# A two-layer decoder on one core: the second weight row's sum moved into an accumulating DMA, and the squared-ReLU tiles handled in pairs

## The chip, the cores and the metric

The kernel runs on one core of one Trainium2 chip. The metric is the device time of one execution in microseconds (us), as the median of several runs. Before the change it is 2010.63 us over three runs, from 2010.59 to 2010.78.

## The reference

Two layers work on `x` of 256 tokens by 2048 channels, in float32. Each layer has a token mixer (causal pooling in layer 0, differential attention in layer 1) beside a memory cross-attention, an output projection, and then the block that the change touches, a squared-ReLU MLP over 8192 hidden channels:

```python
def squared_relu_mlp(h, w1, w2):
    z = jax.nn.relu(h @ w1)          # w1: 2048 x 8192
    return (z * z) @ w2              # w2: 8192 x 2048

    # in each layer i:
    x = x + jnp.concatenate([token_out, mem_out], axis=-1) @ w_out[i]
    x = x + squared_relu_mlp(rms_norm(x, ffn_norm[i]), w_ff1[i], w_ff2[i])
```

## The kernel before

**Split products.** Every weight is read from memory in float32 and split on the chip into a high part, rounded to the type that TensorE takes (`hi_ring`, a cast by ScalarE, L178), and the rest (`lo_ring`, a subtraction by VectorE, L181). Activations are split in the same way. A product of two split matrices takes three products of the parts; the one of the two rests is left out. `hi_ring` and `lo_ring` are rings of six slots of 512 columns, so the splits can be only a few blocks ahead of TensorE.

**The order of loading and splitting.** The program runs twice. The first, dry pass writes down the order in which weights are used; `Plan.close` makes of it the list of preparations (`prep`) and the list of loads. Class `Feed` then loads rows of 1024 columns through SyncE's queue (`load`, L122) and splits jobs up to three ahead of the one in use (`_prepare`, L190). A job `N` is a plain block of 512 columns. A job `S` belongs to a slab of ff2.

**The MLP** (`ffn`, L730). 64 tiles of ff1 (`up_tile`, 128 hidden channels each) are made one after the other in one PSUM bank, `x_bank`. Each is evicted, its two halves are added, then ReLU, square and split follow. Two neighbouring tiles and 1024 columns of ff2 make a slab: a 2 by 2 by 2 block product, computed with seven products in place of eight (a fast scheme for 2 by 2 matrices). 60 slabs in each layer are computed between the ff1 tiles, in four jobs `S0` to `S3` each (`slab_jobs`, `product`, L862); `due` fixes how many jobs come before which tile. The last eight slices of ff1 go into eight tiles of the output in plain form (`down_tile`).

The scheme needs sums on both sides. On the side of the activations, VectorE builds four sums of 128 columns for each pair (L792 to L795), which are split in a buffer of their own (`sit`, L800 and L803), beside the four original blocks (`z`, L772 and L776). On the side of the weights, with the slab's two rows called r0 and r1, each of two halves:

- `t1` = left half of r0 + left half of r1. A plain DMA brings the first, an accumulating DMA that GpSimd issues (L153) adds the second in flight (`first_sum`).
- Step `K`, first of the slab: VectorE makes r1's left half = `t1` - r1's right half (L204). Only the right half of r1 is loaded (L143).
- `S0` splits r0, `S1` splits `t1`, `S2` splits r1; behind the split of `S0`, VectorE turns both halves of r0 into differences (L218, 1024 columns), and `S3` splits those.

r0 and r1 of a slab with an even number lie in a pool of three tiles (`rows`), r1 of an odd one in `spare`, a part of `room`. So a tile is loaded again only when the split that reads it, two slabs before, has been done.

**Order on the engines.** Within what the program writes, a scheduler puts the instructions of each engine in a fixed order, and each engine works through its own in that order: an instruction that waits holds up all behind it on its engine.

Of the kernel before, what the change touches and what calls it, by code (L numbers as in the profile page):

```python
# [55 lines left out]
class Plan:  # L56
# [13 lines left out]
    def close(self):  # L70
        prep = []
        for job in self.jobs:

            if job[0] == "S" and job[2] == 0:
                prep.append(("K", job[1]))
            prep.append(job)
# [4 lines left out]
        for p in prep:  # L81
            if p[0] == "K":
# [16 lines left out]
class Feed:  # L99
# [22 lines left out]
    def load(self, upto):  # L122
        while self.lp < min(upto, len(self.plan.loads)):
# [18 lines left out]
            else:  # L142
                self.nc.sync.dma_start(t[:, 512:1024], self.wst[h, :, 512:1024])  # L143
# [46 lines left out]
    def _prepare(self, p):  # L190
        sub, add = self.nc.vector.tensor_sub, self.nc.vector.tensor_add
# [11 lines left out]
        if p[0] == "K":  # L203
            one = sub(rb[:, 0:512], t1, rb[:, 512:1024])  # L204
# [10 lines left out]
        if p[2] == 0:  # L215
            t2 = rb[:, 0:512].unsqueeze(1).to_broadcast([P, 2, 512])
            two = ra.rearrange("p (a c) -> p a c", a=2)
            sub(two, t2, two)  # L218
        if p[2] == 1:
            self.t1_of[p[1] % len(self.t1)] = None  # L220
        if p[2] == 3:
# [70 lines left out]
def program(ctx, tc, plan, dry, xT, memT, par, lam, cst, wst, yT):  # L292
# [437 lines left out]
    def ffn(l, xs, tags, done):  # L730
# [7 lines left out]
        z = sp.tile([P, NK, 512], F32R, tag=tags[0], name=f"z{l}")  # L738
        room = sp.tile([P, 8192], F32, tag=tags[1], name=f"room{l}")
        sums_in = sp.tile([P, 4, 1024], F32R, tag="big", name=f"sit{l}")  # L740
        staged = sp.tile([P, 2048], F32, tag="big2", name=f"stage{l}")
        sit = [sums_in[:, j, :] for j in range(4)]
        stage = [staged[:, T * j : T * j + T] for j in range(8)]
        sums = [room[:, 512 * j : 512 * j + 512] for j in range(2)]
        feed.t1 = [room[:, 1024 + 512 * j : 1536 + 512 * j] for j in range(3)]
        outs = [room[:, 2560 + 512 * j : 3072 + 512 * j] for j in range(2)]
# [7 lines left out]
        z_done, sit_done = set(), set()  # L754
        z_free = {j: True for j in range(NK)}
        sit_free = [True] * 4

        def evict(ps):
            x = outs[cnt[0] % 2]
            cnt[0] += 1  # L760
            return x, nc.scalar.copy(x, ps)  # L761
# [4 lines left out]
        def convert(j):  # L766
            a = stage[j % 8]
            k = j % NK

            def high():  # L770
                z_free[k] = False
                nc.scalar.copy(z[:, k, 0:T], a)  # L772
                at(1, low)

            def low():
                nc.vector.tensor_sub(z[:, k, T : 2 * T], a, z[:, k, 0:T].bitcast(F32))  # L776
                z_done.add(j)

            when(lambda: z_free[k], high)
            if j % 2 == 0:  # L780
                return
            i = j // 2

            def ready():
                return j in z_done and j - 1 in z_done and sit_free[i % 4]

            def combine():
                sit_free[i % 4] = False
                a11, a21 = stage[2 * i % 8][:, 0:P], stage[2 * i % 8][:, P:T]
                a12, a22 = stage[(2 * i + 1) % 8][:, 0:P], stage[(2 * i + 1) % 8][:, P:T]  # L790
                s1, s2, s3, s4 = (sums[i % 2][:, c * P : c * P + P] for c in range(4))
                nc.vector.tensor_add(s1, a21, a22)  # L792
                nc.vector.tensor_sub(s3, a11, a21)
                nc.vector.tensor_sub(s2, s1, a11)
                nc.vector.tensor_sub(s4, a12, s2)  # L795
                at(1, sums_high)
                at(2, sums_low)

            def sums_high():
                nc.scalar.copy(sit[i % 4][:, 0:512], sums[i % 2])  # L800

            def sums_low():
                nc.vector.tensor_sub(  # L803
                    sit[i % 4][:, 512:1024], sums[i % 2], sit[i % 4][:, 0:512].bitcast(F32)
                )
                sit_done.add(i)

            when(ready, combine)

        def up_tile(i, ps, between=None):  # L810
# [5 lines left out]
            y, out = evict(ps)  # L816
            if i == 3 and not dry:
                feed.cast_behind = [out.ins.name] * 3
            at(1, lambda: nc.vector.tensor_add(y[:, 0:T], y[:, 0:T], y[:, T : 2 * T]))
            d = 5 if i == 2 else 2  # L820

            def relu():
                one = nc.scalar.activation(y[:, 0:T], y[:, 0:T], AF.Relu)
                if i == 2 and not dry:
                    feed.order(one, feed.last_cast.ins.name)

            at(d, relu)

            def square():
                assert i < 8 or i - 8 in z_done  # L830
                nc.scalar.activation(stage[i % 8], y[:, 0:T], AF.Square)
                at(1, lambda: convert(i))

            at(d, square, 2)

        def down_tile(n, ps, between=None):
            ks = range(56, 64)
            assert all(k in z_done for k in ks)
            if n >= 3:
                c_tile(ps, "w_ff2", l, n, ks, z)  # L840
# [5 lines left out]
            a_part(ps, "w_ff2", l, n, ks, z, between=between)  # L846
            x, _ = evict(ps)
# [24 lines left out]
        def slab_jobs(g, i, again, end):  # L872
# [9 lines left out]
            def plain(c, t):  # L882
                assert k + c in z_done
                zk = z[:, (k + c) % NK, :]
# [753 lines left out]
```

## Time and profile before

| | |
|---|---|
| median of 3 runs | 2010.63 us (2010.59 to 2010.78) |
| span of the profiled execution | 2010.7 us |
| TensorE busy | 1999.0 us, 99% |
| VectorE busy | 1779.2 us, 88% |
| ScalarE busy | 1525.3 us, 76% |
| GpSimd busy | 157.1 us, 8% |
| TensorE's mean granted clock | 0.999 |
| moved by DMA | 422.19 MB, 210 GB/s |

The profile is of one execution. PE is TensorE's matmuls, PEld its weight loads, DVE VectorE, ACT ScalarE, POOL GpSimd, SP SyncE. A row of a group of instructions gives the line, the engine, the operation, the names written and read, shapes and count, then the busy time in us and the mean of one in ns, then the idle time of the engine just before them. A row of waits gives who waited for whom, in us in total, times, and the longest. A row of a window gives its length, and for each engine the busy time with the count of instructions, then the granted clock of TensorE, the share of the DMA engines' time that packets took, and GB/s. The MLP of layer 0 lies at about 257 to 931 us of the span, that of layer 1 at 1336 us to the end.

### The profile page before, as it was taken

To read this page: it belongs to the slowest core of one execution; us is meant where nothing else is said; L and a number is where in the kernel's file an instruction comes from. 1 tells how busy PE (TensorE), PEld (TensorE's weight loads), DVE (VectorE), ACT (ScalarE), POOL (GpSimd) and SP (SyncE) were. 2 spreads that over 40 slices of the span, in tenths; PEclk is the share of its full clock that TensorE was granted. 3 is DMA by queue.
4 is the path that set the end of the run, shared out by engine and by line. 5 is a ranking of instruction groups with operands and counts; after the bars stand their busy time and mean duration, and the time that the engine had idled before them with its cause. 6 is when DMAs were issued, how large, how long until landed. Compare 5 with 4: busy or idle time off the path is not lost.

```text
span 2010.7 us, 31966 instructions
## 1 busy us (share of the span) xinstructions
PE 1999.0 (99%) x10510; PEld 1696.5 (84%) x10510; DVE 1779.2 (88%) x3096; ACT 1525.3 (76%) x2838; POOL 157.1 (8%) x187
## 2 busy tenths in 40 slices
PE   9999999999999999999999999999999999999999
PEld 8888888888888888888888888888888888888877
DVE  8888888989999999999765698878989999999998
ACT  7765577787887888878665699557787878878885
POOL 0001310000000000100000000320000000100000
PEclk9999999999999999999999999999999999999999
DMA  8555576777778777755575533567777777777773
GB/s 319 171 188 195 188 221 208 232 221 229 226 226 240 223 218 234 225 175 175 181 235 194 178 127 126 199 197 229 224 214 233 225 234 223 231 230 231 223 228 124
DMA packets 145030, 422.19 MB, mean 210 GB/s; under 512 B 16352, under 2 KB 19040, under 8 KB 144864
## 3 DMA queue, kind: packets, MB, share of 16 engines
q1 hardware_dynamic: 127440, 388.69, 57.5%
q0 software_dynamic: 17280, 31.46, 9.7%
q8 instruction: 82, 1.34, 0.3%
q14 instruction: 84, 0.69, 0.1%
q10 hardware_dynamic: 144, 0.01, 0.0%
HBM read 418.00 MB, written 2.10 MB: 209 GB/s over the span
## 4 chain that ended last, share of the span: by engine, by line
PE 93%; ACT 3%; DVE 2%; issue 1%; DMA 0%; ACTq 0%; DVEq 0%
PE x_bank L433 21%; PE x_bank L435 11%; PE p L867 9%; PE p L870 9%; PE p L869 9%; PE wo L433 6%; PE wo L435 3%; PE u L433 2%; ACT hi_ring L178 1%; PE ff L433 1%; PE u L435 1%; PE k L469 1%; PE q L467 1%; PE q L469 1%; PE q L468 1%; PE v L468 1%
## 5 line engine op out<-in xcount | busy, mean ns | idle before, releaser
L178 ACT CAST hi_ring<-raw 128x512 fp32r<-128x512 f32 x969 | 593.5, 623 | 267.3 <-PE x_bank L433 61.1
L181 DVE TENSOR_TENSOR lo_ring<-raw,hi_ring 128x512 fp32r<-128x512 f32 x969 | 662.0, 695 | 105.1 <-ACT hi_ring L178 93.5
L433 PE MATMUL x_bank<-fx,hi_ring 128*128 128x512 f32 x1952 | 610.8, 394 | 0.0
L435 PEld LDWEIGHTS x_bank<-fx,lo_ring 128*128 128x128 f32 x1952 | 365.1, 188 | 88.1 <-DVE lo_ring L181 6.1
L181 DVE TENSOR_TENSOR lo_ring<-slab,hi_ring 128x1024 fp32r<-128x1024 f32 x300 | 366.4, 1221 | 50.1 <-ACT hi_ring L178 48.8
L178 ACT CAST hi_ring<-slab 128x1024 fp32r<-128x1024 f32 x300 | 314.6, 1053 | 117.2 <-PE p L869 65.0
L435 PE MATMUL x_bank<-fx,lo_ring 128*128 128x256 f32 x1952 | 384.8, 278 | 1.5 <-DVE lo_ring L181 1.5
L433 PEld LDWEIGHTS x_bank<-fx,hi_ring 128*128 128x128 f32 x1952 | 320.7, 189 | 26.8 <-ACT room L761 1.3
L153 POOL DMA_DIRECT2D room<-in_w x120 | 104.0, 872 | 1139.7 <-DMA room<-in_w 1121.4
L867 PE MATMUL p<-hi_ring,sit 128*128 128x512 f32 x480 | 190.5, 397 | 0.4 <-ACT hi_ring L178 0.2
L869 PE MATMUL p<-hi_ring,sit 128*128 128x512 f32 x480 | 187.9, 391 | 0.0
L870 PE MATMUL p<-lo_ring,sit 128*128 128x512 f32 x480 | 186.5, 391 | 0.2
L433 PE MATMUL wo<-cat,hi_ring 128*128 128x512 f32 x512 | 161.8, 397 | 0.3 <-DVE rc L404 0.3
L181 DVE TENSOR_TENSOR lo_ring<-room,hi_ring 128x512 fp32r<-128x512 f32 x180 | 154.3, 863 | 5.7 <-ACT hi_ring L178 5.6
L178 ACT CAST hi_ring<-room 128x512 fp32r<-128x512 f32 x180 | 138.1, 769 | 19.0 <-PE p L869 9.5
L867 PE MATMUL p<-hi_ring,z 128*128 128x512 f32 x360 | 141.2, 392 | 0.7 <-ACT hi_ring L178 0.7
L869 PE MATMUL p<-hi_ring,z 128*128 128x512 f32 x360 | 140.6, 391 | 0.0
L870 PE MATMUL p<-lo_ring,z 128*128 128x512 f32 x360 | 139.7, 392 | 0.0
L435 PEld LDWEIGHTS wo<-cat,lo_ring 128*128 128x128 f32 x512 | 95.9, 188 | 22.0
L870 PEld LDWEIGHTS p<-lo_ring,sit 128*128 128x128 f32 x480 | 89.8, 188 | 21.8 <-DVE lo_ring L181 2.7
L867 PEld LDWEIGHTS p<-hi_ring,sit 128*128 128x128 f32 x480 | 90.0, 187 | 15.6 <-ACT hi_ring L178 5.8
L435 PE MATMUL wo<-cat,lo_ring 128*128 128x256 f32 x512 | 101.5, 279 | 0.0
(370 smaller groups left out, 3339.9 us busy)
## 6 DMA issues: line engine op xcount, KB each, us to landing
raw<-in_w SPq DMA_DIRECT2D x484, 512.0 KB, 4.3
slab<-in_w SPq DMA_DIRECT2D x120, 512.0 KB, 4.4
room<-in_w SPq DMA_DIRECT2D x180, 256.0 KB, 3.3
room<-in_w POOLq DMA_DIRECT2D x120, 256.0 KB, 5.7
slab<-in_w SPq DMA_DIRECT2D x60, 256.0 KB, 4.3
memraw<-in_mem SPq DMA_DIRECT2D x5, 512.0 KB, 4.5
resid<-in_x SPq DMA_DIRECT2D x8, 256.0 KB, 5.5
out_y<-resid SPq DMA_DIRECT2D x16, 128.0 KB, 1.9
```

Source lines behind the costliest of these rows:

```text
L153: self.nc.gpsimd.dma_start(self.t1[i], right, accum_op=ALU.add)
L178: self.last_cast = self.nc.scalar.copy(hi, src)
L181: low = self.nc.vector.tensor_sub(lo, src, hi.bitcast(F32))
L433: nc.tensor.matmul(ps, hi, xs[:, k, :], start=first and c == 0, stop=False)
L435: nc.tensor.matmul(ps[:, T : 2 * T], lo, xs[:, k, 0:T], start=False, stop=last and c == len(ks) - 1,)
L467: nc.tensor.matmul(ps[t], x[t][1], hi, start=k == 0, stop=False)
L468: nc.tensor.matmul(ps[t], x[t][0], hi, start=False, stop=False)
L469: nc.tensor.matmul(ps[t], x[t][0], lo, start=False, stop=k == NK - 1)
L867: nc.tensor.matmul(ps, a[1], hi, start=new, stop=False, **again)
L869: nc.tensor.matmul(ps, a[0], hi, start=False, stop=False, **again)
L870: nc.tensor.matmul(ps, a[0], lo, start=False, stop=end, **again)
```

## The change

- **Weights.** r1 is loaded whole (L143), and a second accumulating DMA of GpSimd adds its right half onto its left half. The step `K` moves from the head of the slab to behind `S1`, and is now two additions of 512 columns: r0's left half = `t1` + r1's right half, then r0's right half += that. The subtraction over 1024 columns behind `S0` goes. `t1` is set free after `S3` in place of `S1`. Nothing is subtracted any more; signs are moved into the sums of the activations and into the steps that put the seven products together (`close_left`, `finish_banks`, and the places of the banks in `of_job`).
- **Activations.** Two ff1 tiles are evicted side by side into one buffer (`two_y`). One addition, one ReLU and one square of 512 columns serve both. The square is written into a row of eight blocks of 128 columns; three VectorE operations (256, 128 and 128 columns) build the four sums in that row, and one cast and one subtraction split the seven operands that the products use (896 columns; 1024 for the last four pairs, which the plain tiles read too). Six pairs have a place (`z`, `zb`) where before there were 16 single blocks and four groups of sums.

The core of the diff:

```diff
-            if job[0] == "S" and job[2] == 0:
+            prep.append(job)
+            if job[0] == "S" and job[2] == 1:
                 prep.append(("K", job[1]))
-            prep.append(job)
...
-                self.nc.sync.dma_start(t[:, 512:1024], self.wst[h, :, 512:1024])
+                self.nc.sync.dma_start(t, self.wst[h])
+                self.nc.gpsimd.dma_start(t[:, 0:512], self.wst[h, :, 512:1024], accum_op=ALU.add)
...
         if p[0] == "K":
-            one = sub(rb[:, 0:512], t1, rb[:, 512:1024])
-            if p[1] % PER_PART:
-                self.order(one, self.last_low.ins.name)
+            one = add(ra[:, 0:512], t1, rb[:, 512:1024])
+            self.order(one, self.last_low.ins.name)
+            add(ra[:, 512:1024], ra[:, 0:512], ra[:, 512:1024])
...
-        if p[2] == 0:
-            t2 = rb[:, 0:512].unsqueeze(1).to_broadcast([P, 2, 512])
-            two = ra.rearrange("p (a c) -> p a c", a=2)
-            sub(two, t2, two)
-        if p[2] == 1:
+        if p[2] == 3:
             self.t1_of[p[1] % len(self.t1)] = None
...
+            def combine():
+                twice = block(A21).unsqueeze(1).to_broadcast([P, 2, P])
+                nc.vector.tensor_sub(
+                    block(S1, 2).rearrange("p (a c) -> p a c", a=2), twice,
+                    block(A22, 2).rearrange("p (a c) -> p a c", a=2),
+                )
+                nc.vector.tensor_sub(block(S2), block(S1), block(A11))
+                nc.vector.tensor_add(block(S4), block(A12), block(S2))
...
             def high():
-                z_free[k] = False
-                nc.scalar.copy(z[:, k, 0:T], a)
+                pair_free[i % 6] = False
+                nc.scalar.copy(pair(i)[:, 0, 0:n], u[:, 0:n])
...
-            at(1, lambda: nc.vector.tensor_add(y[:, 0:T], y[:, 0:T], y[:, T : 2 * T]))
...
+                nc.scalar.activation(left, left, AF.Relu)
+                u = staged[:, i // 2 % 2, 512:1024].rearrange("p (a c) -> p a c", a=2)
+                nc.scalar.activation(u, left, AF.Square)
```

**VectorE in the middle of the MLP of layer 0, before.** One slab: `slab_6925` is its r0, `slab_6929` its r1, `room_2604` as a source of `lo_ring` is `t1`, `raw_` rows are jobs `N`.

```order
L204 TENSOR_TENSOR slab_6929<-room_2604,slab_6929 128x512
L792 TENSOR_TENSOR room_2604<-stage_2606 128x128
L794 TENSOR_TENSOR room_2604<-room_2604,stage_2606 128x128
L795 TENSOR_TENSOR room_2604<-stage_2606,room_2604 128x128
L181 TENSOR_TENSOR lo_ring<-slab_6925,hi_ring 128x1024
L181 TENSOR_TENSOR lo_ring<-raw_6952,hi_ring 128x512
L218 TENSOR_TENSOR slab_6925<-slab_6929,slab_6925 128x1024
L181 TENSOR_TENSOR lo_ring<-room_2604,hi_ring 128x512
L181 TENSOR_TENSOR lo_ring<-slab_6929,hi_ring 128x1024
L181 TENSOR_TENSOR lo_ring<-raw_6952,hi_ring 128x512
L776 TENSOR_TENSOR z_2603<-stage_2606,z_2603 128x256
```

The same slab in the changed kernel; `slab_6777` is r0, `slab_6781` is r1.

```order
L785 TENSOR_TENSOR stage_2606<-stage_2606 128x256
L789 TENSOR_TENSOR stage_2606<-stage_2606 128x128
L790 TENSOR_TENSOR stage_2606<-stage_2606 128x128
L182 TENSOR_TENSOR lo_ring<-slab_6777,hi_ring 128x1024
L182 TENSOR_TENSOR lo_ring<-raw_6794,hi_ring 128x512
L182 TENSOR_TENSOR lo_ring<-room_2604,hi_ring 128x512
L205 TENSOR_TENSOR slab_6777<-room_2604,slab_6781 128x512
L182 TENSOR_TENSOR lo_ring<-slab_6781,hi_ring 128x1024
L207 TENSOR_TENSOR slab_6777<-slab_6777 128x512
L182 TENSOR_TENSOR lo_ring<-raw_6794,hi_ring 128x512
```

The step `K` (L204 before, L205 and L207 now) has moved from ahead of the split of r0 to behind that of `t1`, and the 1024-wide L218 is gone. The split of r1 is third of the slab's four, as before.

**GpSimd's queue, from the end of layer 0's output projection, before.** L706 and L707 are the squares of the norm, L153 the accumulating DMAs.

```order
L706 TENSOR_TENSOR psq<-resid 128x256
L707 TENSOR_TENSOR acc<-acc,psq 128x256
L153 DMA room_2604<-in_w 128x512 x60
L700 TENSOR_TENSOR acc<-resid 128x256
L706 TENSOR_TENSOR psq<-resid 128x256
```

The same place in the changed kernel: L154 is the accumulation onto `t1`, L144 that onto r1.

```order
L703 TENSOR_TENSOR acc<-acc,psq 128x256
L154 DMA room_2604<-in_w 128x512 x3
L144 DMA room_2604<-in_w 128x512
L154 DMA room_2604<-in_w 128x512
L144 DMA slab_3004<-in_w 128x512
L154 DMA room_2604<-in_w 128x512
L144 DMA room_2604<-in_w 128x512
```

The two kinds take turns in one queue, so an accumulation onto `t1` now stands behind one that waits for r1's plain load to land, and the other way round.

More of the change, by code (lines that the diff above doesn't have):

```diff
@@ L81, in close @@
         for p in prep:
-            if p[0] == "K":
+            if p[0] == "S" and p[2] == 0:
                 self.loads += [("S", p[1], 0), ("S", p[1], 1)]
@@ L753, in ffn, with pair, __getitem__ @@
         cnt = [0]
-        z_done, sit_done = set(), set()
-        z_free = {j: True for j in range(NK)}
-        sit_free = [True] * 4
+        done_pairs = set()
+        pair_free = [True] * 6
+        S1, S3, S2, S4, A12, A22, A11, A21 = range(8)
+        def pair(i):
+            i = i % 6
+            return z[:, i] if i < 4 else z_more[:, i - 4]
+        class Chunks:
+            def __getitem__(self, at):
+                _, k, c = at
+                k = 48 + k
+                half = pair(k // 2)[:, :, 512 + 256 * (1 - k % 2) : 768 + 256 * (1 - k % 2)]
+                if c == slice(None):
+                    return half
+                return half[:, 0 if c.start == 0 else 1, :]
         def evict(ps):
@@ L784, in ready @@
[L784 to L797, printed above, removed]
@@ L799, in sums_high @@
[L799 to L802 removed]
                 nc.vector.tensor_sub(
[L804 removed]
+                    pair(i)[:, 1, 0:n], u[:, 0:n], pair(i)[:, 0, 0:n].bitcast(F32)
                 )
[L806 to L808 removed]
+                done_pairs.add(i)
+            combine()
         def up_tile(i, ps, between=None):
```

109 lines of the change are left out of this document (49 added, 60 removed).

## The prediction

> **What bounds the kernel now.** I read the page first, for the engines' shares.
>
> ```profile
> span 2010.7 us, 31966 instructions
> PE 1999.0 (99%) x10510; PEld 1696.5 (84%) x10510; DVE 1779.2 (88%) x3096; ACT 1525.3 (76%) x2838; POOL 157.1 (8%) x187
> ```
>
> TensorE is busy for 99% of the span, and the change takes no product from it. So the question is how much of its time is idle where the change works. The windows answer it: the MLP of layer 0, the junction behind it, the stretch of low clock that follows, and the MLP of layer 1.
>
> ```profile
> 257.00:902.00 645.00, 643.45 (x3298) 542.27 (x3297) 598.34 (x911) 521.53 (x892) 52.06 (x60) 1.00 0.74 222
> 902.00:934.00 32.00, 29.28 (x195) 25.31 (x193) 31.39 (x64) 25.89 (x52) 0.00 (x0) 1.00 0.39 132
> 934.36:937.77 3.41, 3.41 (x10) 2.63 (x9) 2.80 (x7) 0.99 (x3) 0.00 (x0) 0.50 0.48 154
> 1336.00:1980.00 644.00, 642.67 (x3296) 541.81 (x3295) 598.08 (x910) 520.75 (x891) 51.95 (x60) 1.00 0.74 222
> ```
>
> TensorE's idle time is 645.00 - 643.45 = 1.55 us in the first MLP, 644.00 - 642.67 = 1.33 us in the second, 32.00 - 29.28 = 2.72 us in the junction. At half the clock for 3.41 us it does 1.7 us of work, so 1.7 us are lost there too. All that the change can win is the sum: 1.55 + 1.33 + 2.72 + 1.7 = 7.3 us, 0.36% of the time. The waits of TensorE in these stretches say what holds it (first MLP, junction, second MLP).
>
> ```profile
> PE x_bank L435 <- DVE lo_ring L181: 1.0, 2, 0.6
> PE p L867 <- ACT hi_ring L178: 0.3, 2, 0.2
> ```
> ```profile
> PE k L467 <- DVE room L842: 1.2, 1, 1.2
> PE k L469 <- DVE lo_ring L181: 0.7, 1, 0.7
> PE ff L449 <- DVE lo_ring L181: 0.6, 1, 0.6
> ```
> ```profile
> PE x_bank L435 <- DVE lo_ring L181: 0.8, 2, 0.6
> PE p L867 <- ACT hi_ring L178: 0.6, 3, 0.2
> ```
>
> VectorE is late 1.0 + 0.8 = 1.8 us in the MLPs, ScalarE 0.3 + 0.6 = 0.9 us (where banks are swapped). No wait there is for a DMA.
>
> Is TensorE really full? Its starts in the timeline:
>
> ```profile
> 658.47 0.40 PE L867 MATMUL p<-hi_ring,sit 128*128 128x512 f32 x1
> 658.70 0.39 PE L869 MATMUL p<-hi_ring,sit 128*128 128x512 f32 x1
> 658.93 0.39 PE L870 MATMUL p<-lo_ring,sit 128*128 128x512 f32 x1
> ```
>
> Matmuls of 512 columns start every 0.23 us and overlap; there is no gap to fill. [...] As a rival, TensorE not being full, I give it 0.01, inside the chance of faster.
>
> **The change part by part.** The rows that price it:
>
> ```profile
> L181 DVE TENSOR_TENSOR lo_ring<-slab,hi_ring 128x1024 fp32r<-128x1024 f32 x300 | 366.4, 1221 | 50.1 <-ACT hi_ring L178 48.8
> L178 ACT CAST hi_ring<-slab 128x1024 fp32r<-128x1024 f32 x300 | 314.6, 1053 | 117.2 <-PE p L869 65.0 <-PE x_bank L433 50.0 <-ACT hi_ring L178 1.4
> L218 DVE TENSOR_TENSOR slab<-slab,slab 128x1024 f32<-128x1024 f32 x60 | 73.1, 1218 | 0.0
> L831 ACT ACTIVATE stage<-room 128x256 f32<-128x256 f32 x128 | 54.0, 421 | 2.1
> L776 DVE TENSOR_TENSOR z<-stage,z 128x256 fp32r<-128x256 f32 x128 | 53.6, 419 | 4.7 <-ACT z L772 4.4
> L823 ACT ACTIVATE room<-room 128x256 f32<-128x256 f32 x128 | 53.6, 419 | 17.7 <-DVE room L819 17.2
> L819 DVE TENSOR_TENSOR room<-room 128x256 f32<-128x256 f32 x128 | 53.5, 418 | 0.1
> L772 ACT CAST z<-stage 128x256 fp32r<-128x256 f32 x128 | 52.4, 409 | 2.0
> L803 DVE TENSOR_TENSOR sit<-room,sit 128x512 fp32r<-128x512 f32 x64 | 43.8, 685 | 0.1
> L204 DVE TENSOR_TENSOR slab<-room,slab 128x512 f32<-128x512 f32 x60 | 41.1, 685 | 10.6 <-DMA room<-in_w 10.6
> L800 ACT CAST sit<-room 128x512 fp32r<-128x512 f32 x64 | 39.9, 623 | 0.7 <-DVE room L795 0.5
> L792 DVE TENSOR_TENSOR room<-stage 128x128 f32<-128x128 f32 x64 | 18.3, 286 | 5.5 <-ACT stage L831 5.5
> ```
>
> *Slab, VectorE.* Out goes 1.218 us (L218), in comes a second 512-wide addition like L204, 0.685 us: -0.53 us for each of 120 slabs, -64 us. L204's wait for the accumulating DMA, 10.6 us at the heads of the two MLPs, goes with `K`'s new place; what is late next there is `t1` at `S1`, for which no row shows a wait, so I cost this at nothing.
>
> *Pair, VectorE.* Out: 2 x 0.418 (L819), four sums of 128 columns at 0.286 (L792 and its sisters), 2 x 0.419 (L776), 0.685 (L803), together 3.50 us. In: one addition of 512 columns, 0.685, as L204; sums of 256, 128 and 128 columns, 0.418 + 2 x 0.286; a subtraction of 896 columns, three quarters of the way from 0.685 (512) to 1.221 (1024), 1.09. Together 2.76 us. 64 pairs at -0.74 us: -47 us.
>
> *Pair, ScalarE.* Out: 2 x (0.419 + 0.421 + 0.409) + 0.623 = 3.12 us. In: ReLU and square of 512 columns at 0.623 each, after the cast L800, and a cast of 896 columns between 0.623 and 1.053, 0.95. Together 2.19 us: -0.93 us, -59 us for 64 pairs. Evictions stay two for a pair.
>
> So VectorE falls from 598.34 + 598.08 = 1196 us to 1085 us of 1289 us, from 93% to 84%, ScalarE from 1042 to 983 us, from 81% to 76%. Hardly any of the 111 and 59 us lies on the path: TensorE hides them. What counts is the 1.8 us for which VectorE is late in the MLPs; I take them to go. ScalarE's 0.9 us I leave: a swap of two banks still puts four copies ahead of the next cast, and single instructions on that queue get longer (0.95 where 0.41 and 0.62 stood).
>
> *Junction.* VectorE is busy 31.39 of 32.00 us, and what the change removes lies almost all ahead of that window. What can carry over is its backlog at the window's start, of which this shows one piece:
>
> ```profile
> 902.27 1.05 ACT L178 CAST hi_ring<-room 128x1024 fp32r<-128x1024 f32 x1
> ```
> ```profile
> 904.81 1.22 DVE L181 TENSOR_TENSOR lo_ring<-room,hi_ring 128x1024 fp32r<-128x1024 f32 x1
> ```
>
> The cast ends at 903.32, its subtraction starts at 904.81: 1.5 us behind. Bounds for the junction are 0 and the whole 2.72 + 1.7 us; I take half of the backlog, -0.7 us, since the additions, scalings and splits between 905 and 934 us keep their number and TensorE still waits for the last of them. The clock's fall I leave.
>
> *The DMAs.* Each slab now loads 256 KB more through SyncE's queue and accumulates 256 KB more through GpSimd's. GpSimd's 120 more issues lie on an engine that is busy 52 us of 645, and move past each other, and the first of a layer past the squares of the norm, which come long after its load. What counts is when r1 is ready. Rows: the landing of plain loads of 512 KB (r0, L139), that of accumulations (L153), and one of the slabs whose margin is least.
>
> ```profile
> L139 SPq DMA_DIRECT2D slab<-in_w x120: 327/328/328, 81.6 to 1970.0; - x120
> ...
> DMA to landing us min/median/max: 3.1/4.4/7.5
> ```
> ```profile
> L153 POOL DMA_DIRECT2D room<-in_w x120: 856/865/1226, 257.7 to 1954.3; - x120
> ...
> DMA to landing us min/median/max: 3.6/5.7/8.0
> ```
> ```profile
> 1671.30 0.33 SPq L143 DMA_DIRECT2D slab<-in_w  x1
> ```
> ```profile
> 1683.36 1.05 ACT L178 CAST hi_ring<-slab 128x1024 fp32r<-128x1024 f32 x1 [0.58 <-PE p L869]
> ```
> ```profile
> 1684.47 0.50 PE L867 MATMUL p<-hi_ring,sit 128*128 128x512 f32 x1
> ```
>
> From the issue of r1 to its cast are 12.06 us in this slab, and TensorE takes the result at once, so nothing behind it gives way. The chain needs 4.4 + 5.7 = 10.1 us at the medians, 7.5 + 8.0 = 15.5 at the worst. If it is late, the cast `S2` waits at the head of ScalarE's queue, and behind it stand casts of ff1 blocks and evictions, then TensorE. At the medians 2 us are left, so I cost it at nothing; the upper bound is a rival.
>
> The sum: -1.8 - 0.7 + 0 = -2.5 us, a span of 2008.2 us. The runs' median is 2010.63 for a span of 2010.7, so 2010.63 - 2.5 = **2008.1 us**, -0.12%. A measurement of this kernel can tell about 0.2%, 4.0 us, from no change; so this counts as the same.
>
> **The rivals.**
>
> *The accumulation comes late (slower).* For it speaks the DMA engines' time, on the page:
>
> ```profile
> q1 hardware_dynamic: 127440, 388.69, 57.5%
> q0 software_dynamic: 17280, 31.46, 9.7%
> ```
>
> The change adds 31.46 MB to each: 9.7% once more, and 57.5 x 31.46 / 388.69 = 4.7%, together 14.4% of 2010.7 us = 289 us. All of it falls in the 1289 us of the MLPs: the share there goes from 0.74 to 0.96. If landings stretch in that proportion, the 10.1 us become 10.1 x 0.96 / 0.74 = 13.1 us, 1.0 us more than the tight slab has. At the worst landings, 15.5 us, it is 3.4 us late. A loop of r1 repeats every second slab; if half of the 60 such slabs were late by 1.0 us, that is 30 x 1.0 - 2.5, 2038 us; if a fifth, 12 x 1.0 - 2.5 = +9.5, 2020 us, which I take as its price. It decides from a chain of 12.1 us on. [...] Against it: the share counts the time that packets take while others hold them up, the same engines already move 319 GB/s in the page's first slice against 222 in the MLPs, and 62.9 MB more in 1289 us make only 271. A faster VectorE also frees r1's tile sooner. Chance 0.15.
>
> ```profile
> GB/s 319 171 188 195 188 221 208 232 221 229 226 226 240 223 218 234 225 175 175 181 235 194 178 127 126 199 197 229 224 214 233 225 234 223 231 230 231 223 228 124
> ```
>
> *The junction heals (faster).* If the whole backlog of 1.5 us carries to x_kv's splits, the junction's idle time halves, and the fall of the clock, which follows it, does not come: 1.8 + 1.4 + 1.7 = 4.9, and with ScalarE's 0.9 us 5.8 us: 2004.8 us. [...] For this rival: VectorE's load falls by a tenth. Against it: the junction's work on VectorE has as many instructions as before. Chance 0.27.
>
> *Nothing moves.* TensorE's waits could be set by the order of instructions at the swaps and heads, not by VectorE's load; longer single instructions then eat what shorter queues give. 2010.6 us. For it speaks that VectorE at 93% made TensorE wait only four times in 1289 us. Chance 0.18.
>
> **How the numbers follow.** The forecast has 0.40, and with nothing moved (0.18) makes 0.58 for the same; faster 0.27, slower 0.15. The range begins where all 7.3 us are won, 2003.3 us, and ends where nothing is won and two slabs lose the 1.0 us of the stretched chain, 2010.63 + 2.0 = 2012.6 us. Beyond it lies most of the slower rival, 0.15.
>
> **What would show it.** In the changed profile DVE should stand near 84% in the MLPs and ACT near 76%, with `x_bank <- DVE lo_ring` gone from TensorE's waits. The casts of r1 should show no wait for a DMA of `slab` or `room`; accumulations should land in 6 to 7 us. If ScalarE's `hi_ring` waits for a DMA tens of times, the slower rival has it. If no stretch of clock 0.50 follows the junction, the faster one. A gain of over 7.3 us would mean that TensorE's starts were not as full as I read them.

## The result, and the profile after

The changed kernel takes 2022.07 us, the median of four runs from 2020.88 to 2022.72; the kernel before takes 2010.70 in the same comparison. The ratio is 1.0054, with an interval from 1.0042 to 1.0066: 11.4 us slower, where 2.5 us faster was forecast and the range ended at 2012.6. The page of the changed kernel:

```profile
span 2021.0 us, 31924 instructions
PE 2000.6 (99%) x10510; PEld 1694.8 (84%) x10510; DVE 1701.0 (84%) x2842; ACT 1486.9 (74%) x2582; POOL 260.5 (13%) x307
```

TensorE does the same 10510 matmuls in a longer span, while VectorE and ScalarE have less to do, as forecast. The windows, with the columns as in the prediction (the second MLP begins 4 us later now):

```profile
257.00:902.00 645.00, 639.47 (x3270) 537.12 (x3269) 553.93 (x777) 497.53 (x758) 102.77 (x119) 1.00 0.92 269
...
1340.00:1984.00 644.00, 638.86 (x3267) 536.94 (x3267) 553.42 (x776) 497.36 (x756) 102.19 (x119) 1.00 0.92 269
```

TensorE's idle time in the MLPs has grown from 1.55 and 1.33 us to 645.00 - 639.47 = 5.53 and 644.00 - 638.86 = 5.14 us. Matmuls of 0.39 us start every 0.23 us, so part of each stall is covered by the tail of the last matmul; the whole loss is read from starts. The view of one tile gives the first and last start of each kind of matmul onto it; here the last matmul of each product (`lo_ring` by `z`) onto the banks `p`, layer 0 and layer 1, before:

```profile
L870 PE MATMUL p<-lo_ring,z x180: 389/389/497, 274.9 to 909.0; 128*128 128x512 f32 x180
```
```profile
L870 PE MATMUL p<-lo_ring,z x180: 389/389/479, 1353.5 to 1987.3; 128*128 128x512 f32 x180
```

and after:

```profile
L868 PE MATMUL p<-lo_ring,z x294: 388/389/504, 274.5 to 915.7; 128*128 128x512 f32 x147
```
```profile
L868 PE MATMUL p<-lo_ring,z x294: 389/389/505, 1357.5 to 1998.0; 128*128 128x512 f32 x147
```

The stretch of the products takes 641.2 us where it took 634.1, and 640.5 where it took 633.8: +7.1 and +6.7 us. The junction went the other way. From the last product of layer 0 to the last start on `k` (the products of `x_kv`) it was 1000.8 - 909.0 = 91.8 us:

```profile
L469 PE MATMUL k<-lo_ring,x_kv x96: 389/389/628, 929.8 to 1000.8; 128*128 128x512 f32 x96
```

and is 1004.8 - 915.7 = 89.1 us, without a stretch of low clock:

```profile
L465 PE MATMUL k<-lo_ring,x_kv x96: 389/389/497, 935.7 to 1004.8; 128*128 128x512 f32 x96
```

So 13.8 us were lost in the MLPs and 2.7 won at the junction. TensorE's waits over the whole span say for whom it stood:

```profile
PE x_bank L431 <- DVE lo_ring L182: 3.4, 4, 1.3
PE p L865 <- ACT hi_ring L179: 3.3, 8, 0.6
PE x_bank L429 <- DVE z L799: 2.3, 2, 1.2
PE p L868 <- DVE lo_ring L182: 2.3, 5, 0.6
PE x_bank L429 <- ACT hi_ring L179: 1.2, 2, 0.6
```

The wait `x_bank <- DVE lo_ring`, which was to go, has nearly doubled from 1.0 + 0.8 us, and ScalarE's has grown from 0.9 to 4.5. Followed back, there are four places.

**A late cast.** ScalarE's timeline in slab 42 of layer 0:

```profile
727.88 0.62 ACT L179 CAST hi_ring<-room 128x512 fp32r<-128x512 f32 x1
731.38 1.05 ACT L179 CAST hi_ring<-slab 128x1024 fp32r<-128x1024 f32 x1 [2.89 <-issue]
```

The idle 2.89 us are put down to "issue", to nothing that the profile ties to it. But GpSimd's timeline has the accumulation onto this r1 (L144), and the view of the DMAs its time to landing:

```profile
723.23 0.86 POOL L144 DMA_DIRECT2D slab<-in_w  x1 [8.40 <-DVE room L821]
```
```profile
slab<-in_w POOLq DMA_DIRECT2D x1, 256.0 KB, 8.1
```

It lands at 723.23 + 8.1 = 731.3 us, and the cast starts at 731.38. TensorE loses 0.54 and 0.70 us behind it. Of the 120 casts of r1, 14 start within 0.6 us of such a landing, all 14 in slabs with an even number.

**A swap of banks.** ScalarE's timeline ahead of the cast for slab 44, after and before (L916 and L924 copy banks; L827 and L829 are ReLU and square):

```profile
746.22 0.64 ACT L827 ACTIVATE room<-room 128x512 f32<-128x512 f32 x1
746.75 0.58 ACT L924 COPY room<-p 128x512 f32<-128x512 f32 x1
747.22 0.65 ACT L829 ACTIVATE stage<-room 128x512 f32<-128x512 f32 x1
747.75 0.60 ACT L916 COPY p<-room 128x512 f32<-128x512 f32 x1
...
750.26 1.07 ACT L179 CAST hi_ring<-slab 128x1024 fp32r<-128x1024 f32 x1
```
```profile
743.09 0.43 ACT L823 ACTIVATE room<-room 128x256 f32<-128x256 f32 x1
743.41 1.07 ACT L934 COPY room<-p 128x512 f32<-128x512 f32 x2
...
745.87 0.45 ACT L831 ACTIVATE stage<-room 128x256 f32<-128x256 f32 x1
746.19 0.62 ACT L926 COPY p<-room 128x512 f32<-128x512 f32 x1
```

ReLU and square stand between the same copies in both. They hold ScalarE from 746.22 to 746.75 and from 747.22 to 747.75, 1.06 us, where the single tile's held it from 743.09 to 743.41 and from 745.87 to 746.19, 0.64 us. TensorE's stall behind the cast (from start to start, above the usual distance) has grown from 0.32 to 0.74 us, by the same 0.42.

**The closing of the left half**, VectorE in slab 52 (L945 to L951 put the products together, L205 and L207 are `K`):

```profile
834.87 0.68 DVE L182 TENSOR_TENSOR lo_ring<-room,hi_ring 128x512 fp32r<-128x512 f32 x1
835.48 0.68 DVE L945 TENSOR_TENSOR room<-room,p 128x512 f32<-128x512 f32 x1
...
839.08 0.68 DVE L951 TENSOR_TENSOR room<-room,p 128x512 f32<-128x512 f32 x1
839.67 0.69 DVE L182 TENSOR_TENSOR lo_ring<-raw,hi_ring 128x512 fp32r<-128x512 f32 x1
```

Seven additions stand in a row between two splits, 4.2 us, and TensorE stalls 1.45 us for the second one (0.76 us at this place before).

**The last pair.** The chain to the first output tile of layer 0:

```profile
904.41 1.52 DVE lo_ring L182 x2
...
906.07 1.23 DVE z L799
...
907.34 0.50 PE x_bank L429
```

TensorE waits for the subtraction over all 1024 columns of the pair: 1.34 us from start to start, in layer 1 1.33. Before, no wait at these tiles was for the pair; the longest stall, 0.41 us, was for a split of weights.

### The profile page after: what moved, and what is told of

It reads as the page before. It is cut to its first block, busy times and chain, and to the rows that moved or that the text cites. A ratio compares the mean times of both kernels' runs of the same rounds, so it can differ in the third digit from the quotient of the medians.

```text
span 2021.0 us, 31924 instructions
## 1 busy us (share of the span) xinstructions
PE 2000.6 (99%) x10510; PEld 1694.8 (84%) x10510; DVE 1701.0 (84%) x2842; ACT 1486.9 (74%) x2582; POOL 260.5 (13%) x307
## 3 DMA queue, kind: packets, MB, share of 16 engines
q0 software_dynamic: 34560, 62.93, 18.4%
q8 instruction: 82, 1.34, 0.3%
## 4 chain that ended last, share of the span: by engine, by line
PE 90%; ACT 5%; DVE 3%; issue 1%; DMA 1%; DVEq 0%; ACTq 0%; POOLq 0%
PE x_bank L429 20%; PE x_bank L431 10%; PE p L868 8%; PE p L865 8%; PE p L867 8%; PE wo L429 6%; PE wo L431 3%; ACT hi_ring L179 2%; PE u L429 2%; DVE lo_ring L182 1%; PE ff L429 1%; PE u L431 1%; PE q L463 1%; PE q L465 1%; PE q L464 1%
## 5 line engine op out<-in xcount | busy, mean ns | idle before, releaser
L865 PE MATMUL p<-hi_ring,z 128*128 128x512 f32 x588 | 231.8, 394 | 2.8 <-ACT hi_ring L179 2.5
L867 PE MATMUL p<-hi_ring,z 128*128 128x512 f32 x588 | 229.9, 391 | 0.0
L868 PE MATMUL p<-lo_ring,z 128*128 128x512 f32 x588 | 227.6, 393 | 0.4 <-DVE lo_ring L182 0.4
L154 POOL DMA_DIRECT2D room<-in_w x120 | 104.5, 876 | 580.3 <-DMA room<-in_w 564.6
L144 POOL DMA_DIRECT2D slab<-in_w x60 | 51.9, 865 | 783.8 <-DVE mm_max L652 352.6
L868 PEld LDWEIGHTS p<-lo_ring,z 128*128 128x128 f32 x588 | 110.0, 188 | 29.6 <-DVE lo_ring L182 6.6
L865 PEld LDWEIGHTS p<-hi_ring,z 128*128 128x128 f32 x588 | 110.3, 188 | 20.4 <-ACT hi_ring L179 6.4
L867 PEld LDWEIGHTS p<-hi_ring,z 128*128 128x128 f32 x588 | 110.5, 188 | 13.7
L868 PE MATMUL p<-lo_ring,zb 128*128 128x512 f32 x252 | 99.7, 396 | 2.0 <-DVE lo_ring L182 1.9
```

What stands on the lines that cost most here:

```text
L144: self.nc.gpsimd.dma_start(t[:, 0:512], self.wst[h, :, 512:1024], accum_op=ALU.add)
L154: self.nc.gpsimd.dma_start(self.t1[i], right, accum_op=ALU.add)
L865: nc.tensor.matmul(ps, a[1], hi, start=new, stop=False, **again)
L867: nc.tensor.matmul(ps, a[0], hi, start=False, stop=False, **again)
L868: nc.tensor.matmul(ps, a[0], lo, start=False, stop=end, **again)
```

## The experiments

The twelve runs. "Layer 0" and "layer 1" are the stretches of the products, "junction" the time from the last product to the last start on `k`, all read as above from one profiled execution of each kernel; ratios are to the kernel before, measured beside them.

| kernel | median us | ratio and interval | layer 0 | junction | layer 1 |
|---|---|---|---|---|---|
| before | | | 634.1 | 91.8 | 633.8 |
| the change | 2022.07 | 1.0054 (1.0042-1.0066) | 641.2 | 89.1 | 640.5 |
| no_second_accumulation | 2019.49 | 1.0036 (1.0023-1.0049) | 638.6 | 89.9 | 638.1 |
| weights_part_alone | 2018.07 | 1.0029 (1.0017-1.0041) | 639.1 | 90.6 | 636.4 |
| pairs_alone | 2027.57 | 1.0078 (1.0065-1.0090) | 640.5 | 91.7 | 640.7 |
| last_pair_plain_first | 2021.73 | 1.0052 (1.0039-1.0066) | 639.6 | 91.1 | 638.3 |
| r1_loaded_first | 2019.09 | 1.0041 (1.0028-1.0054) | 638.4 | 89.5 | 638.0 |
| pair_cast_held_in_swaps | 2024.27 | 1.0067 (1.0054-1.0079) | 641.1 | 89.6 | 642.4 |
| closing_spread | 2021.33 | 1.0055 (1.0041-1.0068) | 640.8 | 89.7 | 638.9 |
| four_mended | 2013.76 | 1.0016 (1.0007-1.0025) | 634.8 | 91.4 | 635.3 |
| last_pair_only_in_layer_1 | 2012.92 | 1.0010 (1.0002-1.0019) | 636.4 | 89.0 | 634.9 |
| five_mended | 2009.29 | 0.9992 (0.9983-1.0000) | 632.5 | 92.2 | 632.7 |
| before_closing_spread | 2011.00 | 1.0001 (0.9992-1.0010) | 633.3 | 90.9 | 633.5 |
| weights_part_mended | 2005.85 | 0.9975 (0.9966-0.9985) | 632.5 | 89.9 | 631.4 |

### The parts and the late casts

**no_second_accumulation**

```diff
                 self.nc.sync.dma_start(t, self.wst[h])
-                self.nc.gpsimd.dma_start(t[:, 0:512], self.wst[h, :, 512:1024], accum_op=ALU.add)
```

> The changed kernel without the accumulating DMA onto r1 (the sum of r1's halves is left out, so the products are made of other numbers; every engine's instructions stay). Theory A, the accumulation comes late: the two MLPs lost 6.8 + 6.7 us, all because the cast of r1 waits for the DMA, so the time falls by 13 us, to about 2009. Theory B, the pair's long instructions (ReLU, square, cast and subtraction of 512 to 1024 columns in one piece) stand in front of the weight splits: no change, 2022. My own reading of the stalls lies between: the casts that follow within 0.6 us of a landing explain some 3 us of the 13, so 2019.

The stretches fall by 2.6 and 2.4 us: that is what the second accumulation costs. Theory A is left with 5 of 13.8 us, theory B is wrong as the only cause, and the reading between them, 2019, is met. Of the stalls that remain, those at slabs 28, 36, 44, 48, 49, 52 and at the last pair have the same size within 0.02 us in both layers (one of 0.34 us at slab 12 stands in layer 0 alone); those that went differ between layers and executions. That is how the two kinds are told apart here: the stalls put down to the order of instructions repeat themselves within 0.02 us, those put down to the transfers do not.

**weights_part_alone**: the kernel before with the weights part of the diff; the sums get the signs that fit it.

```diff
-                nc.vector.tensor_add(s1, a21, a22)
-                nc.vector.tensor_sub(s3, a11, a21)
+                nc.vector.tensor_sub(s1, a21, a22)
+                nc.vector.tensor_sub(s3, a21, a11)
...
-                nc.vector.tensor_sub(s4, a12, s2)
+                nc.vector.tensor_add(s4, a12, s2)
```

> The weights part of the change alone, on the single tiles and separate sums of the kernel before. Theory A: all the loss is here, 2020 or more, and the stalls behind a late cast of r1 are found again. Theory B: no loss here; VectorE has 64 us less work, so 2008 to 2011. Mixed: some 3 us of late casts, less 2.5 us for the shorter junction, 2011.

TensorE's waits in layer 0:

```profile
PE p L863 <- ACT hi_ring L179: 4.1, 6, 2.2
PE x_bank L431 <- DVE lo_ring L182: 2.0, 3, 1.6
```

The 2.2 us are one late cast of r1, the 1.6 us the closing. Behind that late cast the granted clock is 0.50 from 530.82 to 534.23 us in this execution (its mean is 0.999), so the 639.1 us of layer 0 hold that as well. The single runs go from 2015.2 to 2020.8 us. All three readings missed the time: some 6 us of loss are here. The late casts that theory A asked for are found.

**pairs_alone**: the changed kernel with the weights part of before.

```diff
+                nc.vector.tensor_add(block(S1), block(A21), block(A22))
+                nc.vector.tensor_sub(block(S3), block(A11), block(A21))
+                nc.vector.tensor_sub(block(S2), block(S1), block(A11))
+                nc.vector.tensor_sub(block(S4), block(A12), block(S2))
```

> The pairing of the ff1 tiles alone, on the weight sums of the kernel before (the four sums are four operations, since their signs are the old ones). Theory A: nothing lost, 2008 to 2010. Theory B: nearly all the loss, 2018 to 2022: 1.3 us at each of the two last pairs, and stalls of 0.4 to 0.8 us at the swaps.

Theory B's direction, and more than it said: 15.4 us. The last pair costs 1.34 us here too, slabs 36, 44 and 49 cost 0.76, 0.80 and 0.90, and stalls come at the head and behind the closing that the whole change does not have. The losses of the two parts don't add up to that of the change (6 + 15 against 11): in the MLP of layer 0 VectorE is busy 580 us here and 554 in the change, and the lighter weights part may make room for the pairs' bursts; that was not tried by itself. The stall at the closing (slab 52) goes with the weights part: it is 0.58 us in this run, without the move of `K`, and 1.74 us in weights_part_alone, with it.

**r1_loaded_first**

```diff
-                self.loads += [("S", p[1], 0), ("S", p[1], 1)]
+                self.loads += [("S", p[1], 1), ("S", p[1], 0)]
```

> The changed kernel with r1 of each slab loaded ahead of its r0, so that r1 takes the tile that comes free first, some 2.1 us earlier in the slabs with an even number, where all late casts were. Theory 'chain': the accumulation is late because two transfers one behind the other start too late; two more us cure nearly all of the late casts, and the time is that of the run without the second accumulation, about 2019.5. Rival 'bandwidth': the DMA engines (0.92 busy in the MLPs) are the limit, what starts earlier lands no earlier, 2022.

The chain theory holds. The stretches are those of the run without the accumulation (638.4 and 638.0 against 638.6 and 638.1), two casts of r1 in place of 14 come within 0.6 us of the landing (0.53 and 0.55 us) with no stall of TensorE behind them, and the DMA engines are as busy as they were:

```profile
257.00:902.00 645.00, 641.15 (x3281) 539.34 (x3280) 556.25 (x782) 500.05 (x760) 102.83 (x119) 1.00 0.92 269
```

At the same share of 0.92 and 269 GB/s, with r1 started earlier, no stall of TensorE stands behind those two. In the even slabs the median from the issue of r1's plain load to its cast rose from 15.3 to 18.4 us, while the chain itself, from that issue to the landing of the accumulation, got no shorter (a median of 12.7 us, 11.7 in the change). The rival 'bandwidth' is not what decided: the same DMA engines with the same load were in time. r1 of an even slab stood behind r0 in SyncE's queue, and r0 took the tile that came free first.

### The order of instructions

In the edits below `at(n, ...)` puts off what the program writes by n ticks, steps of a counter in the program (`now`), and so moves it behind other instructions in an engine's order.

**last_pair_plain_first**

```diff
+            def plain_high():
+                pair_free[i % 6] = False
+                nc.scalar.copy(pair(i)[:, 0, 512:1024], u[:, 512:1024])
+                at(1, plain_low)
...
+            if i == 31:
+                when(lambda: pair_free[i % 6], plain_high)
+            else:
+                combine()
```

> The changed kernel, but in the last pair of each layer the four plain blocks are cast and split (512 columns) ahead of the four sums, which follow. Theory B: TensorE's waits for that pair's subtraction, 1.2 us in each layer, go: 2019.5. Rival: the next wait (a split of weights behind it on VectorE) takes their place: 2021.5 to 2022.

The wait for the pair is gone from both layers and the stretches are 1.6 and 2.2 us shorter, but the time hardly moves: the junction takes 91.1 us in place of 89.1. TensorE's waits there, in this run and in the change:

```profile
PE k L463 <- DVE room L855: 1.2, 1, 1.2
PE ff L445 <- DVE lo_ring L182: 0.7, 2, 0.6
PE k L465 <- DVE lo_ring L182: 0.7, 1, 0.7
```
```profile
PE k L465 <- DVE lo_ring L182: 1.2, 1, 1.2
PE k L463 <- DVE room L840: 0.4, 1, 0.4
```

The reading is that VectorE works off what the junction would wait for while TensorE stands for the last pair; the run last_pair_only_in_layer_1 below tries it. This is the rival of the expectation, in layer 0.

**pair_cast_held_in_swaps**

```diff
-                at(1, lambda: when(lambda: pair_free[i % 6], high))
+                at(1, lambda: when(lambda: pair_free[i % 6] and now[0] > swap_at[0], high))
...
-                    at(3 if j == 3 else 2, lambda: swap(j, 1 - g))
+                    d = 3 if j == 3 else 2
+                    at(d, lambda: swap(j, 1 - g))
+                    swap_at[0] = now[0] + d
```

> The changed kernel, but the cast of a pair (896 columns, L795) is held back while a swap of banks is under way. Theory 'pair on top of swap': the stalls at the swaps of slabs 36 and 49 and at slab 44 (0.92 + 0.57 + 0.74 = 2.2 us in each layer) lose half or more, 2019.5. Rival 'swap by itself': fourteen copies of 0.49 us hold up the casts of weights whatever the pair does, 2022.

The stall of 0.76 us at slab 36 is gone and one of 0.31 us at slab 29 stands for that of 0.40 at slab 28; those at 44 and 49 stay (0.75 and 0.57): the pair's cast is not what stands in that swap. The total is worse; in the profiled execution 17 casts of r1 came late, one by 4.1 us. With the late casts still in, no total can answer such a question; single places can.

**closing_spread**

```diff
+                sub(left["c12"], left["v"], left["u"])
...
-                sub(v, v, u)
-                add(u, u, banks[6])
+                restore(3, 0)
+
+                def rest():
+                    one = sub(v, v, u)
+                    if not dry:
+                        feed.order(one, feed.any_low.ins.name)
+                    add(u, u, banks[6])
+                    restore(6, 0)
+
+                at(2, rest)
```

> The changed kernel, but in the closing of the left half (slabs 51 and 52) one operation comes two jobs earlier and the last two come two ticks later, behind the split of an ff1 block. Theory 'additions of K among the closing': the stall of 1.45 us there falls to 0.75 or less, as it was before, -0.7 to -1.5 us in each layer: 2020 to 2020.7. Rival: the next split is late instead, 2022.

At the place itself the theory holds; in TensorE's waits of layer 0 the row of 1.7 us has shrunk to

```profile
PE x_bank L432 <- DVE lo_ring L182: 0.4, 1, 0.4
```

What is left is the wait at slab 49. In the time the gain can't be seen beside 17 late casts (1.0055).

**four_mended**: the four edits together.

> The changed kernel with r1 loaded first, the pair's cast held in swaps, the closing spread, and the last pair's plain blocks first. If the loss of 6.8 + 6.7 us is the sum of these four causes (late casts 2.5, swaps 2.2 at most, closing 1.0, last pair 1.0 to 1.6 us in each layer), some 5 to 6 us of each layer come back; of that 2 us were lost again behind the junction when the last pair was mended alone. So 2012 to 2014, near the kernel before. If the causes hide one another, 2017 or more.

As the sum asked: 2013.76 us, and stretches within 0.7 and 1.5 us of those before. TensorE's waits in layer 0:

```profile
PE p L882 <- ACT hi_ring L179: 1.0, 2, 0.6
PE x_bank L432 <- DVE lo_ring L182: 0.6, 2, 0.4
```

**last_pair_only_in_layer_1**: as four_mended, with `i == 31 and l == 1`.

> The four cures, but the last pair's plain blocks go first in layer 1 alone. If the junction gave back what the cure won in layer 0, the MLP of layer 0 gets 1.6 us longer, the stretch to the last product of x_kv 1.6 to 2 us shorter, and the time stays at that of the four cures (about 2012 to 2014). Rival: the cure was worth its 1.6 us in layer 0 and the time is that much longer.

Layer 0 takes 636.4 in place of 634.8 us, the junction 89.0 in place of 91.4, the time stays, 1.0010 against 1.0016, each within the other's interval. The wait for the last pair costs nothing in layer 0; it stands in for waits of the junction.

**five_mended**

```diff
-            at(1 + d, square)
+            def square_when():
+                at(1, square) if d and now[0] <= swap_at[0] else square()
+
+            at(1 + d, square_when)
```

> The changed kernel with the first three cures (r1 first, cast held in swaps, closing spread; the last pair as the change made it), and the pair's ReLU and square also held back one tick where a swap is under way. Theory 'pair on top of swap': the stalls left at slabs 44 and 49 (0.75 + 0.57 us) fall by half or more; the MLP takes about 1.6 us more than the four cures leave for the last pair, less 0.7 us or more: 644.5 us. Rival 'swap by itself': they stay, 645.5 us.

The kernel that ran has the last pair's cure as well, other than the expectation says, so it is to be held against four_mended: 2.3 and 2.6 us less, more than the theory asked. Of TensorE's waits in layer 0 the view lists one:

```profile
PE ff L446 <- DVE lo_ring L182: 0.2, 1, 0.2
```

The stalls at 44 and 49 are gone, that at 48 is 0.24 in place of 0.61. So it was ReLU and square, 0.42 us longer as a pair, on top of the copies.

**before_closing_spread**: the same for the kernel before.

```diff
-                sub(v, v, u)
-                sub(u, u, banks[6])
+                restore(5, 0)
+
+                def rest():
+                    one = sub(v, v, u)
+                    if not dry:
+                        feed.order(one, feed.any_low.ins.name)
+                    sub(u, u, banks[6])
+                    restore(6, 0)
+
+                at(2, rest)
```

> The kernel before, with the last two operations of the closing two ticks later and nothing else: its stall of 0.76 + 0.24 us there goes, -0.8 us in each layer, -1.6 us. If it gains as much as the mended weights part, the change itself brings nothing. Rival: another split is late, 0.

Nothing: 1.0001. The stall of 0.76 us goes, and one of 1.35 us comes one slab later, behind VectorE's 599 of 645 us. The rival has it.

**weights_part_mended**: weights_part_alone with r1_loaded_first and closing_spread.

> The weights part alone (single tiles and separate sums as before), with r1 loaded ahead of r0 and the closing spread. If the late casts and the additions among the closing were all that the weights part cost, the stalls of 3 us and 1.7 us in each layer go and VectorE's lighter load is left: the MLPs take 641 to 642 us each in place of 643.3 and 642.8 before, and the time is 1 to 4 us under that of the kernel before. Rival: the stalls of 0.33 to 0.5 us at the swaps are made of the weights part too and stay, no change against before.

2005.85 us, ratio 0.9975 (0.9966 to 0.9985): faster than both kernels. TensorE's waits in layer 0:

```profile
PE p L864 <- ACT hi_ring L179: 1.0, 4, 0.3
PE x_bank L432 <- DVE lo_ring L182: 0.4, 2, 0.2
PE x_bank L430 <- DVE z L773: 0.3, 1, 0.3
```

The rival's stalls stay (0.3 to 0.5 us at slabs 20, 28, 44 and 48), and the stretches are still 1.6 and 2.4 us under those before. Since the spread closing brings the kernel before nothing, I put the gain down to the weights part, once its transfer is in time; the order of loading was not tried on the kernel before, whose TensorE shows no wait for a load. five_mended, measured beside the same runs of the kernel before, takes 3.4 us more than this: even mended, the pairs bring nothing here.

## Why the prediction was wrong

- **What bounds it** was read rightly: TensorE's starts were full, one every 0.23 us, and no version won more than the 7.3 us (the largest gain is 5.2).
- **The prices of the parts** were right, and led nowhere. The cast and the subtraction of 896 columns were estimated at 0.95 and 1.09 us; they take 0.948 and 1.089:

```profile
L799 DVE TENSOR_TENSOR z<-stage,z 128x896 fp32r<-128x896 f32 x40 | 43.6, 1089 | 17.3 <-ACT z L795 17.3
L795 ACT CAST z<-stage 128x896 fp32r<-128x896 f32 x40 | 37.9, 948 | 24.3 <-DVE stage L790 24.0
```

  In the MLPs VectorE is busy 1107 us where 1085 was forecast, ScalarE 995 where 983 was. The sum took rows at their full length, but in the row of additions above one of 0.68 us starts every 0.60 us, so an instruction that goes frees about 0.08 us less than its row says. For the 254 instructions that VectorE lost that makes some 20 us, an estimate, and so most of its difference.
- **"What counts is the 1.8 us for which VectorE is late in the MLPs; I take them to go"**: this step failed. It read lateness as load. VectorE's load in the MLPs fell by 89 us and TensorE's wait `x_bank <- lo_ring` rose from 1.8 to 3.4 us, because TensorE waits at a few places where the order is fixed: in each layer 1.3 us of it stand in the closing, where `K`'s two additions joined five others, and 0.4 at slab 49, behind a swap. The prediction followed the move of `K` through the plain slab and did not look where it lands in the closing. Its rival 'nothing moves' had the mechanism, the order of instructions and longer single ones, but gave it a price of nothing and not a loss.
- **"ScalarE's 0.9 us I leave"**: the sentence itself says that single instructions get longer, and then gives it no price. The swap's rows had it: 0.42 us more between the same copies. With the pair's cast, this is the part at the swaps: the stalls at slabs 28, 36, 44, 48 and 49 of layer 0 are together 3.1 us, where before two of 0.32 us stood, at slabs 20 and 44.
- **The last pair** had no term at all. It costs 1.3 us in each layer, which in layer 0 the junction gives back.
- **The DMAs, "at the medians 2 us are left, so I cost it at nothing"**: failed as well. Both transfers landed about as forecast (r1's plain loads at a median of 5.1 us, accumulations at 6.5), and the least time from issue to cast was still 12.0 us. But the cost was taken from a sum of medians, while plain loads of r1 take up to 8.0 us and accumulations up to 9.2; in slab 42 of layer 0 one of 8.0 and one of 8.1 us met, a chain of 16.6 us with the 0.6 us between them. The rival named the mechanism and the number of slabs (12; 14 were found), and priced each at 1.0 us; they cost 5.0 us together, 0.36 each: in slab 42 ScalarE stood for 2.89 us and TensorE lost 1.24 of them, and behind some of the 14 TensorE does not stall at all. The forecast share of the DMA engines, 0.96, was nearly met (0.92). Beside it the accumulations' median rose from 5.7 to 6.5 us, but that alone does not make a cast late: with an earlier start at the same share, in r1_loaded_first, the stretches are as short as without the accumulation (638.4 and 638.0 us against 638.6 and 638.1).
- **The junction**: -0.7 forecast, -2.7 measured. Part of that is the fall of the clock that did not come. The prediction left it out of the forecast and counted it as 1.7 us in its bound and its rival; that is too much for the time, since what follows then waits less. The rival has the fall gone once the junction idles less, which was the author's assumption; no run shows that this decides it (see the last section). The run before_closing_spread has the same three waits and no fall, and its junction takes 90.9 us against 91.8, 0.9 us less; a fourth wait stands there that the profile of the kernel before does not have:

```profile
PE tc_x L502 <- DVE acc L718: 0.5, 1, 0.5
```

  The reason given for the -0.7, less backlog on VectorE, is not it in the change: with the last pair cured, most of the gain is lost again.
- **The sum**: late casts 2.8 + 2.5 (to r1_loaded_first), the other three cures 3.6 + 2.7 (from r1_loaded_first to four_mended), ReLU and square 2.3 + 2.6 (to five_mended) are together 16.5 us: the 13.8 lost, and the 1.6 and 1.1 us by which five_mended lies under the kernel before. How the 6.3 us of the three cures divide was not timed free of late casts. The stalls in the traces of r1_loaded_first and four_mended tell it for layer 0: about 1.5 us go at the closing, 1.6 at the last pair, 0.9 with the pair's cast in the swaps, together somewhat more than the 3.6 by which the stretch falls.
- **The base** was off by 1.8 us: in every run here the time is 1.7 to 1.9 us above the span, so the profiled execution of before, with a span of 2010.7, was a longer one than the median, and the idle times were read from it.

## What to carry to other kernels

Where one engine is full, relief of the others is worth only what they are late (here 2.7 us before the change, in two MLPs of some 640), and here they were late at a few places: swaps, closings, heads and tails. Look up there, row by row, what a longer instruction or a moved step stands in front of, and price that. For a chain of two transfers, set the long landings against the least margin, and see first what the load stands behind in its queue: one line that put r1 ahead of r0 took back what the late casts cost. And mend what varies from run to run first; only then do small edits show.

## What the runs showed of the hardware

The fall of the clock behind the junction is not a fixed part of a kernel. In 57 runs of the kernel before, beside the experiments, 12 have a mean granted clock of 0.999 and a median of 2011.89 us, the other 45 one of 1.000 and 2010.95. The profile that the prediction used was of the first kind. In it the clock is 0.50 from 934.36 to 937.77 us, for 3.41 us; the rows of 2 us around this place:

```profile
926.00:928.00 2.00, 1.97 (x15) 1.53 (x13) 2.00 (x7) 1.65 (x5) 0.00 (x0) 1.00 0.27 109
928.00:930.00 2.00, 1.47 (x11) 1.47 (x12) 2.00 (x5) 0.78 (x3) 0.00 (x0) 1.00 0.01 4
930.00:932.00 2.00, 0.80 (x4) 0.32 (x4) 1.66 (x5) 2.00 (x5) 0.00 (x0) 1.00 0.74 262
932.00:934.00 2.00, 1.31 (x5) 0.74 (x5) 2.00 (x6) 1.41 (x4) 0.00 (x0) 1.00 0.00 0
934.00:936.00 2.00, 2.00 (x5) 1.59 (x6) 2.00 (x5) 0.74 (x2) 0.00 (x0) 0.59 0.22 37
936.00:938.00 2.00, 2.00 (x7) 1.54 (x6) 1.16 (x3) 0.84 (x2) 0.00 (x0) 0.56 0.75 256
```

The last two of these rows hold 12 matmuls of TensorE, the two from 938 to 942 us, with the clock at 1.00 again, hold 20. The run weights_part_mended has the same waits of 1.2, 0.7 and 0.6 us there as the kernel before, and no fall:

```profile
924.00:926.00 2.00, 1.50 (x11) 1.07 (x9) 2.00 (x6) 1.66 (x5) 0.00 (x0) 1.00 0.13 51
926.00:928.00 2.00, 1.94 (x13) 1.68 (x13) 2.00 (x5) 0.77 (x2) 0.00 (x0) 1.00 0.20 37
928.00:930.00 2.00, 0.80 (x4) 0.50 (x4) 1.65 (x5) 1.71 (x5) 0.00 (x0) 1.00 0.57 225
930.00:932.00 2.00, 1.31 (x6) 0.78 (x5) 2.00 (x5) 1.70 (x4) 0.00 (x0) 1.00 0.00 0
932.00:934.00 2.00, 2.00 (x11) 1.62 (x10) 2.00 (x6) 0.76 (x2) 0.00 (x0) 1.00 0.42 94
```

TensorE is idle for 2.45 us in the first four rows of either. In before_closing_spread it is idle for 2.45 us as well, from 926 to 934 us, with the clock at 1.00 throughout; in pairs_alone it is 2.08 us, from 936 to 942 us, and the clock is 0.53 and 0.62 in the two rows that follow. So the sum of idle time does not decide it. Of the fourteen profiles, three have a clock under 1.00 in the rows behind the junction, up to 966 us: the kernel before, pairs_alone, and five_mended (0.57 and 0.57 from 932 to 936 us). What decides it was not shown.
